# Five of six blocks of attention's value projection by seven quarter products, with the values kept in DRAM between

## The chip, the cores and the metric

One core of one Trainium2 chip runs a whole two-layer block in one launch. The metric is the device time of that launch in microseconds, as the median of several runs. The five engines are TensorE (PE, with its weight loads as PEld), VectorE (DVE), ScalarE (ACT), GpSimd (POOL) and SyncE (SP, which here only issues DMAs).

## The reference

512 tokens of width 1024 pass through two layers: an HGRN mixer with a SwiGLU FFN, and dilated attention with a SwiGLU FFN, each with normalisation and modulation. The change touches the second layer's attention. There one projection gives queries, keys and values for three dilation groups of eight heads of 128:

```python
proj = (u @ w_in).astype(jnp.float32).reshape(B, S, N_GROUPS, 3, ATT_HEADS, ATT_HEAD_DIM)
for gi, (window, dilation) in enumerate(DILATED_GROUPS):
    q = apply_partial_rope(proj[:, :, gi, 0], cos, sin) * scale
    k = apply_partial_rope(proj[:, :, gi, 1], cos, sin)
    v = proj[:, :, gi, 2]
    o_g, lse_g = dilated_group_attention(q, k, v, window, dilation)
```

So the values are three products of 512 x 1024 by 1024 x 1024. Each group attends in windows of 128 positions, group 0 over neighbouring tokens, groups 1 and 2 over every fourth and every sixteenth token; the groups' outputs are merged by a softmax over their log-sums and projected out. Everything is float32.

## The kernel before

**Products.** Float32 products are made from three products of fp32r parts (`three`, L415 to L419): each operand is split into a high part (an ACT cast) and a low part (a DVE subtraction), and high x high, high x low, low x high are added up in PSUM. The activations `u` of a layer lie split in `uh` and `ul`. A weight tile of 1 MB (128 x 2048) is loaded by SP into one of two `raw` buffers and split into one of three `hi` and `lo` buffers (class `Stream`, L84 and L85, or in two pieces, L105 and L106). The order of the loads is a list written out beforehand (`items`); `weave` puts pieces of the modulation (`ada`, eight DVE operations per vector half, L245) between the weights.

**The FFN's stage of seven products.** In both FFNs most of the first matrix is multiplied by quarters in the manner of Strassen and Winograd: operands are cut in four, and seven products of quarters with sums made on DVE and POOL replace eight (`token_sums`, `seven_products`, L726 to L881). There the sums of the tokens are made under two plain blocks.

**The attention's values.** A value block is one group and one half of the heads: 512 tokens by 1024 by 512 columns, made as four token tiles of 8 x 3 products of 512 columns. Six such blocks exist. The first, group 0 and heads 0 to 3, is multiplied inside `ffn(0, ...)`, at the end of the first layer: token tile by token tile between the last normalisations (`open_attention` returns `v_prod`; its ACT copy is L1532). Groups 1 and 2 of the first half follow (`tok_proj`), and those of the second half, with group 0, come after the queries and keys of head 4. For groups 1 and 2 the result goes through DRAM (`bounce`, L1343 and L1345, POOL's queue) to be read back with a stride of four tokens. The values stay in SBUF as `V[g]`, 512 columns at a time.

**The heads.** For every head and group a query and a key block (`block`, 24 products of 512 columns each) is multiplied; `fl` (class `Fillers`) runs scores, softmax, merging, flips and value products (`pv_r`, `pv_n`) of the earlier head between them at fixed half steps (`fl.tick`).

**What sets the order.** Outside marked blocks a scheduler orders each engine's queue by program order and readiness. Inside `with tc.manual_schedule(engines=ORDERED)` the queues of PE, ACT, DVE and POOL hold that block's operations in the order in which they are written; `ffn`'s end, from the last weight tiles on, is such a block. Engines run their own queues in order and wait for one another by semaphores. PSUM has eight banks: four tagged `mm`, two `a`, two `b`.

## Time and profile before

| | us |
|---|---|
| median of three runs | 1513.37 (1510.27 to 1513.59) |
| the profiled execution, its time | 1511.66 |
| its span from the first to the last instruction | 1509.9 |
| end of the first layer's FFN and first value block | 645 to 680 |
| two value blocks, then the heads | 680 to 1136 |
| mean granted TensorE clock | 0.997 of full speed |

A row of a timeline gives the start, the time taken, engine, line, operation, written tile `<-` read tiles, shape and count; in square brackets stands how long the engine had been idle before and whose end released it. Times are from the start of the span. A row by windows gives the stretch, its length, busy time and instructions of PE, PEld, DVE, ACT and POOL, the granted clock, the DMA share and GB/s. Matmuls are pipelined: their durations overlap, and the distance between starts is what one costs.

### The profile page before, as it was taken

To read this page: it belongs to the slowest core of one execution; us is meant where nothing else is said; L and a number is where in the kernel's file an instruction comes from. 1 tells how busy PE (TensorE), PEld (TensorE's weight loads), DVE (VectorE), ACT (ScalarE), POOL (GpSimd) and SP (SyncE) were. 2 spreads that over 40 slices of the span, in tenths; PEclk is the share of its full clock that TensorE was granted. 3 is DMA by queue.
4 is the path that set the end of the run, shared out by engine and by line. 5 is a ranking of instruction groups with operands and counts; after the bars stand their busy time and mean duration, and the time that the engine had idled before them with its cause. 6 is when DMAs were issued, how large, how long until landed. Compare 5 with 4: busy or idle time off the path is not lost.

```text
span 1509.9 us, 23161 instructions
## 1 busy us (share of the span) xinstructions
PE 1495.6 (99%) x9111; PEld 1307.1 (87%) x9111; DVE 1032.7 (68%) x1764; ACT 692.8 (46%) x1107; POOL 255.9 (17%) x232
## 2 busy tenths in 40 slices
...
GB/s 305 179 174 132 162 140 168 112 62 134 110 106 107 104 210 212 165 56 203 183 144 141 115 111 112 209 181 58 84 34 79 103 94 112 110 104 154 194 111 56
DMA packets 209502, 201.23 MB, mean 133 GB/s; under 512 B 7096, under 2 KB 167024, under 8 KB 208880
## 3 DMA queue, kind: packets, MB, share of 16 engines
...
q10 hardware_dynamic: 512, 0.35, 0.1%
...
## 4 chain that ended last, share of the span: by engine, by line
PE 87%; DVE 6%; POOL 2%; issue 2%; ACT 2%; DMA 1%; DVEq 0%; POOLq 0%; ACTq 0%; SPq 0%
PE ps_mm L417 19%; PE ps_mm L419 19%; PE ps_mm L418 19%; PE ps_b L417 3%; PE ps_b L419 3%; PE ps_b L418 3%; PE ps_a L419 3%; PE ps_a L417 3%; PE ps_a L418 3%; PE ps_mm L1165 1%; DVE loq L795 1%; POOL raw L775 1%; PE ps_a L1617 1%; PE ps_a L1165 1%; PE ps_mm L223 1%
## 5 line engine op out<-in xcount | busy, mean ns | idle before, releaser
L417 PE MATMUL ps_mm<-uh,hi 128*128 128x512 f32 (+1 forms) x784 | 290.2, 370 | 0.0
L419 PE MATMUL ps_mm<-uh,lo 128*128 128x512 f32 (+1 forms) x784 | 288.2, 368 | 0.0
L418 PE MATMUL ps_mm<-ul,hi 128*128 128x512 f32 (+1 forms) x784 | 287.3, 366 | 0.0
L85 DVE TENSOR_TENSOR lo<-raw,hi 128x2048 fp32r<-128x2048 f32 x74 | 174.5, 2358 | 149.0 <-ACT hi L84 148.8
L84 ACT CAST hi<-raw 128x2048 fp32r<-128x2048 f32 x74 | 141.4, 1911 | 155.1 <-DMA raw<-in_ffn_w_out_dram 50.8
L417 PEld LDWEIGHTS ps_mm<-uh,hi 128*128 128x128 f32 x784 | 147.4, 188 | 31.7 <-issue 8.4
L419 PEld LDWEIGHTS ps_mm<-uh,lo 128*128 128x128 f32 x784 | 147.6, 188 | 23.5
L418 PEld LDWEIGHTS ps_mm<-ul,hi 128*128 128x128 f32 x784 | 147.5, 188 | 22.5
L791 ACT CAST hiq<-raw 128x1024 fp32r<-128x1024 f32 x72 | 72.4, 1051 | 72.2 <-DVE raw L779 70.9
L417 PE MATMUL ps_mm<-hi,oh 128*128 128x512 f32 x240 | 94.0, 392 | 0.2 <-ACT oh L413 0.2
L418 PE MATMUL ps_mm<-lo,oh 128*128 128x512 f32 x240 | 93.6, 390 | 0.0
L245 DVE SCALAR_TENSOR_TENSOR shared<-raw,cond,shared 128x512 f32<-128x512 f32 x98 | 73.4, 749 | 27.7 <-DMA raw<-in_ada_w_dram 26.2
L795 DVE TENSOR_TENSOR loq<-raw,hiq 128x1024 fp32r<-128x1024 f32 x72 | 84.9, 1219 | 0.0
L775 POOL TENSOR_TENSOR raw<-raw 128x512 f32<-128x512 f32 x36 | 57.9, 1608 | 105.8 <-DVE loq L771 45.7
L419 PE MATMUL ps_mm<-hi,ul 128*128 128x512 f32 x192 | 74.9, 390 | 0.0
L418 PE MATMUL ps_mm<-lo,uh 128*128 128x512 f32 x192 | 74.7, 389 | 0.0
L417 PE MATMUL ps_mm<-hi,uh 128*128 128x512 f32 x192 | 73.4, 390 | 0.0
L779 DVE TENSOR_TENSOR raw<-raw 128x1024 f32<-128x1024 f32 x36 | 44.1, 1225 | 40.9 <-POOL raw L775 40.9
L419 PE MATMUL ps_mm<-hi,ol 128*128 128x512 f32 x176 | 68.5, 389 | 0.0
L825 POOL TENSOR_TENSOR shared<-shared 128x256 f32<-128x256 f32 x36 | 30.3, 840 | 206.1 <-DVE shared L824 206.1
L247 POOL PARTITION_ALL_REDUCE shared<-shared x12 | 40.6, 3380 | 133.6 <-DVE shared L245 123.7
L417 PE MATMUL ps_mm<-sums,hiq 128*128 128x256 f32 x216 | 59.7, 276 | 0.0
...
## 6 DMA issues: line engine op xcount, KB each, us to landing
raw<-in_ada_w_dram SPq DMA_DIRECT2D x40, 1024.0 KB, 5.1
...
raw<-in_ffn_w_out_dram SPq DMA_DIRECT2D x22, 1024.0 KB, 4.9
raw<-in_hgrn_w_in_dram SPq DMA_DIRECT2D x12, 1024.0 KB, 5.3
raw<-in_attn_w_in_dram SPq DMA_DIRECT2D x12, 1024.0 KB, 5.0
raw<-in_ffn_w_in_dram SPq DMA_DIRECT2D x8, 1024.0 KB, 5.0
...
```

The lines of the kernel that those rows point to most:

```text
L84: self.nc.scalar.copy(hi, t)
L85: self.nc.vector.tensor_sub(lo, t, hi.bitcast(F32))
L245: dve.scalar_tensor_tensor(a, r[:, k], sc, a, op0=OP.mult, op1=OP.add)
L247: pool.partition_all_reduce(a, a, P, bass.bass_isa.ReduceOp.add)
L417: pe.matmul(ps, ah, bh, start=start, stop=False)
L418: pe.matmul(ps, ah, bl, start=False, stop=False)
L419: pe.matmul(ps, al, bh, start=False, stop=stop)
L775: pool.tensor_add(r[:, 2], r[:, 2], r[:, 0])
L779: dve.tensor_tensor(r[:, 0:2], r[:, 0:3:2], r[:, 1:2].broadcast_to((P, 2, 512)), op=OP.add)
L791: act.copy(hi, src)
L795: dve.tensor_sub(lo, src, hi.bitcast(F32))
L825: pool.tensor_add(W[:, 3], W[:, 3], W[:, 5])
```

## The change

The first block (group 0, heads 0 to 3) stays plain, but its result goes to DRAM. The other five, the `UNITS`, are made directly after it, in a stage of their own (`values`) that continues the hand-ordered block at the end of `ffn(0, ...)`. Tokens, inner dimension and columns are each cut in two; seven products p1 to p7 of 256 tokens by 512 by 256 columns replace eight. The sums of token quarters (`full_sum`, `less`, `less_both`, `t_parts`: T0 to T3) are built in the first unit. Every unit sums its weight quarters (S1 on POOL, S2 to S4 on DVE), splits seven quarters, and adds the products up with two ACT copies, six DVE operations and one POOL operation. Its two weight tiles are loaded together, one into `raw`, one into a buffer of its own; the split parts use the `hi` and `lo` buffers. Each result of 1 MB is stored to a DRAM tile `vals[g, half]` from POOL's queue. The heads then fetch the values for two heads at a time, three loads from POOL's queue, with the stride of four tokens for groups 1 and 2; two sets of buffers are held. `tok_proj` and its `bounce` are gone, the pieces of the next weight tile at the end of `ffn` too, and the modulation pieces are woven in from the first head on, one per 1.6 items instead of one per 2.

```diff
--- before.py
+++ after.py
+TPAD = 112
...
+ADA_AT = (0, 1.6)
...
+    def load_unit(self, other):
+        i = self.loaded
+        if i < len(self.items) and self.items[i][0] == "unit":
+            first, second = self.items[i][1]
+            self.raw[i] = [self.pool.tile([P, 2048], F32, name=f"raw{i}", tag="raw", bufs=self.raws),
+                           other.tile([P, 2048], F32, name=f"other{i}", tag="other", bufs=2)]
+            for t, src in zip(self.raw[i], (first, second)):
+                self.nc.sync.dma_start(t.rearrange("p (a b) -> p a b", a=4), src)
+            self.loaded += 1
+    def unit(self):
+        assert self.items[self.done][0] == "unit"
+        self.done += 1
+        return self.raw.pop(self.done - 1)
     def fill(self):
...
-        while self.loaded < len(self.items) and sum(map(real, range(self.done, self.loaded))) + real(self.loaded) <= self.raws:
+        while self.loaded < len(self.items) and self.items[self.loaded][0] != "unit" and sum(map(real, range(self.done, self.loaded))) + real(self.loaded) <= self.raws:
...
+        UNITS = ((1, 0), (2, 0), (0, 1), (1, 1), (2, 1))
...
-        at = []
-        order = []
-        for hd in range(NH):
-            if hd == 0:
-                for g in range(3):
-                    order.append(("v", g, 0))
-                    at += av(g, 0)
-            for g in range(3):
-                order.append(("qk", g, hd))
-                at.append(aqk(g, hd))
-            if hd == 4:
-                for g in range(3):
-                    order.append(("v", g, 1))
-                    at += av(g, 1)
-        items += weave(at, ada_seq((1, 2), (1, 4), (1, 3)), 6, 2)
+        items += av(0, 0) + [("unit", [w for _, w in av(*unit)]) for unit in UNITS]
+        items += weave([aqk(g, hd) for hd in range(NH) for g in range(3)], ada_seq((1, 2), (1, 4), (1, 3)), *ADA_AT)
...
-                    for hi_f, lo_f in st.pieces(2, True):
-                        hi_f()
-                        lo_f()
-                    st.fill()
                     v_prod(vw, 2, range(8))
                     v_prod(vw, 3, range(8))
-                turns.close()
+                    turns.close()
+                    nxt[2]()
...
-        def tok_proj(dst, via=None, ticks=()):
-            ws = [st.take(), st.take(1)]
-            bounce = None if via is None else fresh(dpool, [S, 512], "bounce", 2)
-            for t in range(NT):
-                ps = bank("mm")
-                for kt in range(KT):
-                    whi, wlo = ws[kt // 4]
-                    w = slice((kt % 4) * 512, (kt % 4 + 1) * 512)
-                    three(ps, nat(uh[:, kt])[t], nat(ul[:, kt])[t], whi[:, w], wlo[:, w], kt == 0, kt == KT - 1)
-                if via is None:
-                    act.copy(dst[:, t], ps)
-                else:
-                    m = via[t % len(via)]
-                    act.copy(m, ps)
-                    pool.dma_start(bounce[t * P:(t + 1) * P], m)
-            if via is not None:
-                pool.dma_start(dst, bounce.rearrange("(l r) d -> l r d", r=4))
-                if t in ticks:
-                    fl.tick()
...
-        oT, V, store = [], [], []
         scr = dpool.tile([NH, 2, S, 2], F32, name="scr")
+        vals = {(g, hf): dpool.tile([S, 512], F32, name=f"vals{g}{hf}") for g in range(3) for hf in range(2)}
         heads = {}
         L4 = lambda a: a.rearrange("p (l r) -> p r l", r=4)
+        vx = ExitStack()
+        room_of = {}
+        def out_of(unit):
+            pool.dma_start(vals[unit].rearrange("(t p) d -> p t d", p=P), room_of[unit])
 
         def open_attention():
 
-            ctx.enter_context(hx)
-            otp = hx.enter_context(tc.tile_pool(name="a_ot", bufs=1))
-            oT.extend(heads_of(otp))
-            store.append(otp)
-            hx.enter_context(cx)
-            vp = cx.enter_context(tc.tile_pool(name="a_v", bufs=1))
-            V.extend(vp.tile([P, NT, 512], F32, name=f"V{g}") for g in range(3))
+            va = vx.enter_context(tc.tile_pool(name="a_val", bufs=1))
+            room_of["pool"] = va
             banks = {}
+            dst = room_of[0, 0] = fresh(va, [P, NT, 512], "vals", 2)
+            for _ in range(2):
+                st.load_unit(va)
...
-                    act.copy(V[0][:, t], banks[t])
+                    act.copy(dst[:, t], banks[t])
...
+        def values():
+            va = room_of["pool"]
+            vb = vx.enter_context(tc.tile_pool(name="a_sums", bufs=1))
+            sums_t = vb.tile([P, TPAD + 8 * 1024], F32R, name="sums_a")[:, TPAD:]
+            K4 = lambda t: t.rearrange("p (k n) -> p k n", k=4)
+            Q = lambda t, c: t.rearrange("p (k n) -> p k n", k=4)[:, :, c * 256:c * 256 + 256]
+            H2 = lambda a: a.rearrange("p (a n) -> p a n", a=2)
+            th, tl = [[K4(sums_t[:, o + k:o + k + 1024]) for k in range(0, 4096, 1024)] for o in (0, 4096)]
+            rooms = [vb.tile([P, NT, 512], F32, name="room_a"), fresh(va, [P, NT, 512], "vals", 2)]
+            full = [K4(r.rearrange("p a n -> p (a n)")[:, o:o + 1024]) for r in rooms for o in (0, 1024)]
+            u_of = lambda r, c: [tuple(x[:, 4 * r + k, c * 256:c * 256 + 256] for x in (uh, ul)) for k in range(4)]
+            t_of = lambda i: [(th[i][:, k], tl[i][:, k]) for k in range(4)]
+            US = {"p1": u_of(0, 0), "p2": u_of(1, 0), "p3": u_of(1, 1),
+                  "p5": t_of(0), "p7": t_of(1), "p4": t_of(2), "p6": t_of(3)}
+            def full_sum(k, eng):
+                a = [x[:, 4 * (k // 2):4 * (k // 2) + 4, k % 2 * 256:k % 2 * 256 + 256].bitcast(F32) for x in (uh, ul)]
+                eng.tensor_add(full[k], *a)
+            def less(k, a, b):
+                dve.tensor_sub(full[k], full[a], full[b])
+            def less_both(k, a, b):
+                dve.scalar_tensor_tensor(full[k], full[a], -1.0, full[b], op0=OP.mult, op1=OP.subtract)
+            def t_parts(k):
+                split(th[k], tl[k], full[k])
+            class Unit:
+                def __init__(self, which):
+                    self.which = which
+                    self.steady = which != UNITS[0]
+                    raw = st.unit()
+                    self.q1, self.q0, self.q3, self.q2 = (Q(r, c) for r in raw for c in range(2))
+                    s1 = fresh(va, [P, 1024], "s1", 1)
+                    self.s1 = K4(s1)
+                    self.n = 0
+                    self.at, self.bank = {}, {}
+                def S1(self):
+                    pool.tensor_add(self.s1, self.q0, self.q2)
+                def S3(self):
+                    dve.tensor_add(self.q0, self.q0, self.q1)
+                def S2(self):
+                    dve.tensor_add(self.q1, self.s1, self.q1)
+                def S4(self):
+                    dve.tensor_add(self.q3, self.q3, self.q1)
+                def parts(self, p):
+                    src = {"p1": self.q1, "p2": self.q3, "p3": self.q3, "p4": self.q2, "p5": self.s1, "p6": self.q1,
+                           "p7": self.q0}[p]
+                    if self.n % 2 == 0:
+                        self.tiles = st.part_tiles()
+                    o = self.n % 2 * 1024
+                    self.n += 1
+                    self.at[p] = [t[:, o:o + 1024] for t in self.tiles]
+                    split(*(K4(x) for x in self.at[p]), src)
+                def hold(self):
+                    self.dst = room_of[self.which] = fresh(va, [P, NT, 512], "vals", 2)
+                def run(self, p):
+                    ps = self.bank[p] = bank("a" if p == "p3" and not self.steady else "mm")
+                    hi, lo = self.at.pop(p)
+                    for s in range(2):
+                        tok = slice(s * P, s * P + P)
+                        o = ps[:, s * 256:s * 256 + 256]
+                        for kt in range(4):
+                            w = slice(kt * 256, kt * 256 + 256)
+                            uhi, ulo = US[p][kt]
+                            three(o, uhi[:, tok], ulo[:, tok], hi[:, w], lo[:, w], kt == 0, kt == 3)
+                def to(self, c, r):
+                    return self.dst[:, 2 * c:2 * c + 2, 256 * r:256 * r + 256]
+                def keep2(self):
+                    self.w2 = fresh(va, [P, 512], "w2", 1)
+                    act.copy(self.w2, self.bank["p1"])
+                def keep3(self):
+                    self.w3 = fresh(va, [P, 512], "w3", 1)
+                    act.copy(self.w3, self.bank["p5"])
+                def add4(self):
+                    self.w4 = fresh(va, [P, 512], "w4", 1)
+                    dve.tensor_add(self.w4, self.w2, self.bank["p6"])
+                def add5(self):
+                    self.w5 = fresh(va, [P, 512], "w5", 1)
+                    dve.tensor_add(self.w5, self.w4, self.bank["p7"])
+                def add1(self):
+                    self.w1 = fresh(va, [P, 512], "w1", 1)
+                    pool.tensor_add(self.w1, self.w4, self.w3)
+                def out11(self):
+                    dve.tensor_add(self.to(0, 0), H2(self.w2), H2(self.bank["p2"]))
+                def out12(self):
+                    dve.tensor_add(self.to(1, 0), H2(self.w1), H2(self.bank["p3"]))
+                def out21(self):
+                    dve.scalar_tensor_tensor(self.to(0, 1), H2(self.w5), -1.0, H2(self.bank["p4"]), op0=OP.mult, op1=OP.subtract)
+                def out22(self):
+                    dve.scalar_tensor_tensor(self.to(1, 1), H2(self.w5), -1.0, H2(self.w3), op0=OP.mult, op1=OP.subtract)
+                    out_of(self.which)
+            a = Unit(UNITS[0])
+            a.S1()
+            out_of((0, 0))
+            a.parts("p1")
+            a.parts("p2")
+            full_sum(3, pool)
+            full_sum(2, pool)
+            a.S3()
+            a.S2()
+            a.S4()
+            full_sum(0, dve)
+            full_sum(1, dve)
+            less(0, 0, 1)
+            a.parts("p3")
+            a.parts("p5")
+            t_parts(0)
+            a.hold()
+            a.run("p1")
+            less(1, 3, 1)
+            less_both(3, 0, 3)
+            a.keep2()
+            a.run("p3")
+            t_parts(3)
+            a.parts("p6")
+            less_both(2, 3, 2)
+            a.run("p2")
+            t_parts(2)
+            a.run("p5")
+            a.parts("p4")
+            a.out11()
+            t_parts(1)
+            a.keep3()
+            a.run("p6")
+            a.parts("p7")
+            st.load_unit(va)
+            b = Unit(UNITS[1])
+            b.S1()
+            a.add4()
+            a.add1()
+            b.parts("p1")
+            a.run("p4")
+            b.S3()
+            b.S2()
+            a.run("p7")
+            b.parts("p6")
+            a.out12()
+            b.parts("p5")
+            a.add5()
+            for n in range(1, len(UNITS)):
+                last = a
+                a, b = b, None
+                a.hold()
+                a.run("p1")
+                a.parts("p2")
+                last.out21()
+                a.run("p6")
+                a.S4()
+                a.keep2()
+                last.out22()
+                a.parts("p7")
+                a.run("p5")
+                a.parts("p3")
+                a.add4()
+                a.run("p2")
+                a.keep3()
+                a.add1()
+                a.parts("p4")
+                st.load_unit(va)
+                if n + 1 < len(UNITS):
+                    b = Unit(UNITS[n + 1])
+                    b.S1()
+                else:
+                    st.fill()
+                a.run("p7")
+                a.out11()
+                if b:
+                    b.parts("p1")
+                    b.S3()
+                a.run("p3")
+                a.add5()
+                if b:
+                    b.S2()
+                    b.parts("p6")
+                a.run("p4")
+                a.out12()
+                if b:
+                    b.parts("p5")
+            a.out21()
+            a.out22()
+            vx.close()
...
+        ffn(0, first, h0.close, ((1, 0), open_attention, values), "right")
+        ctx.enter_context(hx)
+        otp = hx.enter_context(tc.tile_pool(name="a_ot", bufs=1))
+        oT = heads_of(otp)
+        hx.enter_context(cx)
+        vp = cx.enter_context(tc.tile_pool(name="a_v", bufs=1))
+        V = {}
+        def fetch(pair):
+            if pair < NH // 2:
+                V[pair] = [fresh(vp, [P, NT, 256], f"V{g}", 2) for g in range(3)]
+                for g in range(3):
+                    src = vals[g, pair // 2][:, pair % 2 * 256:pair % 2 * 256 + 256]
+                    pool.dma_start(V[pair][g], src.rearrange(*(("(l r) d -> l r d",) if g else ("(t p) d -> p t d",)),
+                                                             **({"r": 4} if g else {"p": P})))
...
-            hs = slice((hd % 4) * P, (hd % 4 + 1) * P)
+            hs = slice((hd % 2) * P, (hd % 2 + 1) * P)
...
+            if hd % 2:
+                fetch(hd // 2 + 2)
         fl.n = 0
-        for kind, g, i in order[1:]:
-            if kind == "v":
-                tok_proj(V[g], None if g == 0 else oT[5:] if i else oT[4 * g - 4:4 * g], (0, 1, 2) if i and g == 0 else ())
-                continue
+        for pair in range(2):
+            fetch(pair)
+        for i, g in ((hd, g) for hd in range(NH) for g in range(3)):
...
-        first = mixer_out(oT, store[0], (3, 5), gates.pop((1, 2)), 1, "left", cx.close, tail)
+        first = mixer_out(oT, otp, (3, 5), gates.pop((1, 2)), 1, "left", cx.close, tail)
```

13 lines of the change are left out of this document (6 added, 7 removed).

## The prediction, made before the result was known

> **What bounds the kernel now.** I read the page first: busy shares and the chain that ended last.
>
> ```profile
> PE 1495.6 (99%) x9111; PEld 1307.1 (87%) x9111; DVE 1032.7 (68%) x1764; ACT 692.8 (46%) x1107; POOL 255.9 (17%) x232
> PE 87%; DVE 6%; POOL 2%; issue 2%; ACT 2%; DMA 1%; DVEq 0%; POOLq 0%; ACTq 0%; SPq 0%
> ```
>
> TensorE is busy 99% of 1509.9 us and 87% of the chain. A busy share is an average, so I asked for the stretch that the change rewrites (the attention heads from the second value block on), for one head with modulation work beside it and one without, and for whom PE waits at all.
>
> ```profile
> 686.00:1130.00 444.00, 443.76 (x2198) 375.67 (x2198) 258.21 (x682) 225.52 (x373) 53.06 (x58) 1.00 0.44 131
> 785.52:825.89 40.37, 40.37 (x213) 34.53 (x211) 31.97 (x95) 27.54 (x47) 3.96 (x6) 1.00 0.43 119
> 1054.48:1095.56 41.08, 41.08 (x216) 35.10 (x214) 23.84 (x73) 23.77 (x42) 2.63 (x4) 1.00 0.25 78
> PE ps_b L500 <- DVE xn L494: 2.6, 2, 1.6
> ```
>
> The columns after the length are busy PE, PEld, DVE, ACT, POOL. PE has no hole in 444 us. The longest wait for an engine outside the first microseconds is 1.6 us, once. So here a PE microsecond saved is a microsecond of the kernel, and a PE microsecond lost is one too: there is no old idle time for either to vanish in.
>
> **What the products save.** A plain block is 4 token tiles x 8 x 3 = 96 products of 512 columns. A block by seven products is 7 x 2 token tiles x 4 x 3 = 168 products of 256 columns. The timeline of PE gives the pitch of the first. The second shape already runs in the FFN's stage of seven products, 84 products to a round; POOL's sum at L775 comes once in each round and shows its length.
>
> ```profile
> 722.54 0.39 PE L417 MATMUL ps_mm<-uh,hi 128*128 128x512 f32 x1
> 722.77 0.39 PE L418 MATMUL ps_mm<-ul,hi 128*128 128x512 f32 x1
> 723.00 0.39 PE L419 MATMUL ps_mm<-uh,lo 128*128 128x512 f32 x1
> 432.66 1.62 POOL L775 TENSOR_TENSOR raw<-raw 128x512 f32<-128x512 f32 x1 [1.77 <-DVE spare L771]
> 442.33 1.62 POOL L775 TENSOR_TENSOR raw<-raw 128x512 f32<-128x512 f32 x1 [1.77 <-DVE loq L771]
> 451.99 1.62 POOL L775 TENSOR_TENSOR raw<-raw 128x512 f32<-128x512 f32 x1 [1.77 <-DVE spare L771]
> ```
>
> Starts lie 0.227 us apart, so a plain block takes 96 x 0.2267 = 21.76. A round of 9.665 us is 0.115 per product, so a block by seven takes 168 x 0.115 = 19.32. Five blocks save 5 x 2.44 = 12.2 us if PE never waits. Half of the 512 pitch (0.1133) would make it 13.6; a pitch of 0.1175 would make it 10.1.
>
> **What the seven products ask of the other engines.** Each block needs three weight sums of 1024 columns on DVE, one on POOL, seven splits (a 1024 cast on ACT, a 1024 subtraction on DVE), and seven more adds of 512 (six on DVE, one on POOL) plus two ACT copies. The token sums (four full sums, three differences, four splits) are built once, inside the first block. Prices:
>
> ```profile
> 349.77 4.62 DVE L739 TENSOR_TENSOR sums<-mid,sums 128x1024 fp32r<-128x1024 f32 x4
> 347.02 2.00 ACT L738 CAST sums<-mid 128x1024 fp32r<-128x1024 f32 x2 [12.07 <-DVE mid L735]
> 439.83 0.69 DVE L830 TENSOR_TENSOR shared<-shared,ps_b 128x512 f32<-128x512 f32 x1
> 440.44 1.75 DVE L771 TENSOR_TENSOR loq<-raw,hiq 128x1536 fp32r<-128x1536 f32 x1
> 670.18 1.30 POOL L518 TENSOR_TENSOR ul<-u,uh 128x512 fp32r<-128x512 f32 x1 [0.57 <-ACT uh L517]
> L1345 POOL DMA_DIRECT2D V<-bounce x4: 542/551/556, 705.1 to 992.1; - x4
> L795 DVE TENSOR_TENSOR loq<-raw,hiq x72: 1214/1218/1227, 360.9 to 1373.3; 128x1024 fp32r<-128x1024 f32 x72
> ```
>
> Four DVE operations of 1024 take 4.62 and one alone 1.22, so each adds (4.62 - 1.22) / 3 = 1.13. A DVE add of 512 adds 0.6 (the next one starts 0.61 after 439.83). ACT needs 1.0 for a cast of 1024 (two in 2.00). POOL's 512 is 1.25 to 1.3, so a POOL sum of 1024 is about 2.4 (estimate, doubled less its start). A DMA issue holds POOL 0.55.
>
> **A price that the shares hide.** POOL and DVE do not run such sums side by side:
>
> ```profile
> 670.18 2.56 POOL L518 TENSOR_TENSOR ul<-u,uh 128x512 fp32r<-128x512 f32 x2 [0.57 <-ACT uh L517]
> 671.61 2.21 DVE L106 TENSOR_TENSOR lo<-raw,hi 128x1024 fp32r<-128x1024 f32 x1 [1.85 <-ACT hi L105]
> 439.81 0.74 POOL L825 TENSOR_TENSOR shared<-shared 128x256 f32<-128x256 f32 x1 [5.53 <-DVE shared L824]
> ```
>
> POOL's pair ends at 672.74. DVE's subtraction starts at 671.61 and takes 2.21 instead of 1.22: it ends 1.08 after POOL does, as if nothing had been done before. L830 above, with one operand in PSUM, ran its usual 0.69 beside POOL's L825. So I price a DVE operation with two SBUF operands as waiting until POOL's sum has ended. A reading in which the two only share bandwidth would cost about half of the 6.8 us below, and the sum would be +5 instead of +8.5. The Trainium skill, "SBUF - State Buffer", section "SBUF: two separate sides", calls the shared pair "an exclusive lock, not a bandwidth split" for just these operations; the 2.21 agrees.
>
> **The first block by seven: the term that decides.** All of it lies within a hand-ordered block, and so do the plain block's products and copies ahead of it. In such a block each engine keeps the written order; the trace shows ACT doing so, with only work from outside the block (L84) slipped in:
>
> ```profile
> 673.78 0.59 ACT L1532 COPY V<-ps_mm 128x512 f32<-128x512 f32 x1 [1.25 <-PE ps_mm L419]
> 676.50 1.92 ACT L84 CAST hi<-raw 128x2048 fp32r<-128x2048 f32 x1 [2.13 <-PE ps_mm L419]
> 679.67 0.59 ACT L1532 COPY V<-ps_mm 128x512 f32<-128x512 f32 x1 [1.26 <-PE ps_mm L419]
> 679.25 0.39 PE L419 MATMUL ps_mm<-hi,ul 128*128 128x512 f32 x1
> ```
>
> The last copy comes when PE has finished the plain block: 0.2 us after PE could have begun a next product (679.25 + 0.23). After it in ACT's order comes the cast for p1; DVE's first operation of the stage is the subtraction behind that cast, so DVE, though it has been idle, can begin none of its sums earlier. On POOL the order is first weight sum, then the issue of the finished plain block's store (which waits for the same last copy), then two of the full token sums, then the next block's weight sum. So everything starts when PE runs dry. Up to the last product p7 DVE's queue holds 21 operations: p1, p2, three weight sums, two full sums, a difference, p3, p5, T0, two differences, T3, p6, a difference, T2, p4, an output add, T1, p7. That is 20 x 1.13 + 0.6 = 23.2 us. To it come:
> - that 0.2, the copy 0.5 and p1's cast 1.0, with handoffs: 1.8;
> - POOL's three sums that stand before DVE: the first is granted at the end of the 0.55 issue, 0.4 before p1's subtraction asks, and holds it 2.0; the other two 2.4 each: 6.8;
> - two gaps in which DVE waits for ACT's cast of a token sum it has just made (T3, T2), 1.1 each: 2.2;
> - p7 itself on PE, 24 x 0.115 = 2.7 after its parts.
>
> Sum 23.2 + 1.8 + 6.8 + 2.2 + 2.7 = 36.7 us for a block whose products are 19.3: PE stands still 17.4 us. The order p1, p3, p2 costs nothing by itself, since DVE's queue sets the end.
>
> **The second block** starts with DVE behind: after p7's parts come an add, p1, POOL's add (1.25), two sums, a gap of 1.1 for p6's cast, and p6: 0.6 + 1.13 + 1.25 + 2.26 + 1.1 + 1.13 = 7.5 us, while PE has p7 and p1, 5.4, to do: about 2 us lost, and 1.4 more at p5, whose bank is freed only by the old block's third output. Together 3.4. **Blocks three to five:** DVE has 10 x 1.13 + 6 x 0.6 = 14.9 us of its own, POOL's two sums stand before it for up to 3.65, and one cast gap is 1.1: at most 19.6 against PE's 19.3. The adds from PSUM run beside POOL, so I take 0, with 1 us for all three as the upper end.
>
> **Moved and removed work.**
>
> ```profile
> raw<-in_attn_w_in_dram SPq DMA_DIRECT2D x12, 1024.0 KB, 5.0
> L245 DVE SCALAR_TENSOR_TENSOR shared<-raw,cond,shared 128x512 f32<-128x512 f32 x98 | 73.4, 749 | 27.7 <-DMA raw<-in_ada_w_dram 26.2
> 682.10 2.29 DVE L85 TENSOR_TENSOR lo<-raw,hi 128x2048 fp32r<-128x2048 f32 x1 [1.36 <-ACT hi L84]
> ```
>
> The bounce of strided values through DRAM (16 stores and 4 loads on POOL's queue) becomes 6 stores and 12 loads of 0.55 us; the 12 loads, 3 per two heads, are wanted ten half steps later. A load waits for the last value products of the pair before, and behind it in POOL's queue are the small statistics DMAs; the 20 now there cost PE nothing, so 0, with 1 us if one load blocks them. Weights: a load of 1 MB lands in 5.0 us, and the first two units are asked for as soon as the FFN's room is free, with the plain block's 21.76 us still ahead: 0. Modulation now begins with the first head and comes every 1.6 items instead of every 2: per head 3 / 1.6 - 3 / 2 = 0.4 more pieces of 4 x 0.75 us and a finish of about 1, so DVE 31.97 + 1.6 of 40.4: 83%, 0. Handing over to the first head: its weight split (ACT 1.9, DVE 2.3) can slip into the last block as L84 did above; 0, but 4 us if it is queued behind the last two outputs.
>
> **The clock.** Idle PE has a second price. Columns as before, granted clock third from the end:
>
> ```profile
> 9.00:12.00 3.00, 1.23 (x17) 0.30 (x17) 1.21 (x4) 2.50 (x6) 0.55 (x1) 1.00 1.05 390
> 13.00:16.00 3.00, 2.08 (x12) 2.02 (x11) 2.07 (x8) 2.82 (x7) 1.34 (x3) 0.50 1.17 312
> 16.00:19.00 3.00, 2.98 (x12) 2.29 (x11) 2.90 (x5) 1.29 (x4) 1.00 (x1) 0.50 1.12 339
> ```
>
> After PE had been busy 1.23 of 3 us the clock was 0.5 for the next two windows. Before p3, PE waits 5 us at one stretch and 3 more after a first product, so I expect one such stretch of 0.5. During it PE still waits for DVE, so a slow p3 and p2 cost nothing; if 0.5 held through the second block it would add 6.6. The Trainium skill, "TensorE: Matmul & The Clock Gate", Part 1, gives half rate after "≥1 idle window"; by that rule the clock falls here too, which changes the clock column and not the sum.
>
> **Sum.** Stalls 17.4 + 3.4 = 20.8, less 12.2: +8.6 us. The profiled execution took 1511.66, so 1520.2 by this sum; it lay 1.7 under the median of the three runs, 1513.37, to which the forecast applies: 1522.
>
> **Rivals.**
> 1. *The sums do not meet* (17%). If POOL's sums fall where DVE waits anyway, the 6.8 and most of the second block's loss vanish: the same walk ends at +0.5, 1513.9. For it: POOL's operations lie in DVE's gaps all through the FFN. Against it: here DVE has no gaps.
> 2. *Preparation begins under the plain block* (20%): ACT and POOL take the first casts and the two full sums before the last copy and the store. DVE was idle then, and 7 us of its queue move under the plain block's last products. With the holding by POOL the walk gives +3.3 (1516.7), without it -6.9 (1506.5): the other side. It decides from 4 us of head start if POOL never holds DVE. Against it stands the written order.
> 3. *DVE sets the pace of every block, or the clock stays down* (10%): at 1.22 per 1024 operation instead of 1.13 the walk gives +12.7 (1526); 0.5 through the second block, +15.1 (1528.5).
> 4. *The seven products are not denser than plain ones* is excluded by the FFN's rows, down to the 10.1 above.
>
> **Numbers.** The forecast has 53%, its own range +5 to +12 (1518 to 1525), from the bandwidth reading, the pitch, and the handing over. The range reaches to rivals 1 and 2, mostly, and to the lower end of 3: 1508 to 1528. About 0.3%, 4.5 us, is what a measurement of this kernel can tell from no change. Faster by more: rival 2 without holding and something for an order that I misread, 0.18. Within: rival 1, the rest of 2 and the low edge of the forecast, 0.28. Slower: 0.54.
>
> **What would show it.** In the changed profile: PE waits for DVE right after the plain block, over 10 us in all and in one stretch over 4, and the first block lasts 33 to 39 us; DVE subtractions of 2 us and more where a POOL sum runs; three later blocks of 19.3 with PE dense; heads of 41 us as now; a clock under 1.00 near 690 us. It is wrong if DVE works on token sums before the plain block's last copy, if PE's total wait in the stage is under 12 us, or if heads get longer.

## The result and the profile after

The changed kernel took 1537.49 us (median of four runs, 1534.75 to 1538.27) beside 1512.54 us for the kernel before on the same chip: a ratio of 1.0164, 95% interval 1.0146 to 1.0182. It is slower by 25 us. The forecast was 1522 with a range of 1508 to 1528: the sign was right, the size was not.

The profile's page after, its busy shares and its chain by engine:

```profile
PE 1495.1 (97%) x9471; PEld 1322.2 (86%) x9471; DVE 1108.8 (72%) x1843; ACT 705.0 (46%) x1125; POOL 287.1 (19%) x242
PE 85%; DVE 6%; DMA 3%; ACT 2%; issue 2%; POOL 1%; SPq 0%; POOLq 0%; DVEq 0%; ACTq 0%
```

PE by windows, as in the prediction: about the first unit, the second, the third, and the heads.

```profile
680.10:719.00 38.90, 26.23 (x176) 25.11 (x176) 34.75 (x24) 13.33 (x15) 11.15 (x5) 0.82 0.21 76
719.00:741.00 22.00, 20.68 (x173) 20.27 (x172) 17.74 (x19) 8.69 (x10) 6.26 (x3) 1.00 0.46 154
741.00:760.00 19.00, 19.00 (x167) 19.00 (x165) 15.56 (x16) 7.98 (x10) 6.22 (x3) 1.00 0.49 166
799.00:1160.00 361.00, 350.60 (x1777) 298.40 (x1776) 242.76 (x679) 202.03 (x349) 52.01 (x55) 0.99 0.47 135
```

A hole is a stretch in which PE runs no product. PE, which had none in 444 us before, has them in two places: 12.7 us of the first window's 38.9 and 1.3 us of the second's 22, and 10.4 us of the heads' 361. The units from the third on are dense. By PE's timelines (of the profiled runs) the 25 us split so:

| part | before | after | difference | predicted |
|---|---|---|---|---|
| five value blocks / the stage of seven products | 108.8 | 118.3 | +9.5 | +8.6 |
| the heads and the output projection, value blocks left out | 374.5 | 389.1 | +14.6 | 0 |
| everything else | | | +1 | 0 |

The second row runs from the first query product (722.5 before, 798.4 after) to the first product of the last FFN (1162.3 and 1187.6); of before's 439.8 us, 65.3 are the three value blocks that stood between the heads (3 x 21.76). So the forecast's sum held where it was worked out, and the miss is the step that was set to nothing.

**The stage.** Whom PE waits for there (in all, times, longest):

```profile
PE ps_mm L426 <- DVE loq L422: 7.7, 3, 5.8
PE ps_a L426 <- DVE loq L422: 3.2, 1, 3.2
PE ps_mm L425 <- ACT hiq L421: 2.1, 2, 1.6
PE ps_a L425 <- ACT hiq L421: 1.0, 1, 1.0
```

The timeline at its start (ACT, DVE, POOL), then DVE and POOL 18 us later:

```profile
680.32 0.59 ACT L1520 COPY vals<-ps_mm 128x512 f32<-128x512 f32 x1 [4.85 <-PE ps_mm L427]
680.80 1.05 ACT L421 CAST hiq<-raw 128x1024 fp32r<-128x1024 f32 x1
681.88 6.17 DVE L422 TENSOR_TENSOR loq<-raw,hiq 128x1024 fp32r<-128x1024 f32 x1 [11.03 <-ACT hiq L421]
681.21 1.07 POOL L1501 DMA_DIRECT2D vals<-vals  x1 [5.07 <-ACT vals L1520]
682.32 4.64 POOL L1542 TENSOR_TENSOR vals<-uh,ul 128x1024 f32<-128x1024 f32 x2
699.70 3.40 DVE L1545 TENSOR_TENSOR room_a<-vals,room_a 128x1024 f32<-128x1024 f32 x1
698.73 3.29 POOL L1567 TENSOR_TENSOR s<-raw,other 128x1024 f32<-128x1024 f32 x1 [11.76 <-DVE loq L422]
```

This is the predicted picture: after the last plain copy the cast for p1, DVE idle for 11 us until then, and DVE's first subtraction at 6.17 us instead of 1.22. It ends at 688.05, 1.1 after POOL's two full sums (686.96).

**The heads.** Whom PE waits for there:

```profile
PE ps_a L1810 <- ACT qk L1789: 5.5, 1, 5.5
PE ps_a L1828 <- ACT qk L1789: 3.2, 1, 3.2
PE ps_b L1912 <- ACT pt L1881: 1.7, 1, 1.7
```

The first of these waits, from PE's row back, on the timeline (PE; DVE's end of the rotation, the positional turning of queries and keys; ACT):

```profile
826.82 0.58 PE L1810 MATMUL ps_a<-qk,qk 128*128 128x128 f32 x1 [5.53 <-ACT qk L1789]
815.08 0.68 DVE L1786 TENSOR_TENSOR turning<-turning,rot 64x512 f32<-64x512 f32 x1
823.71 1.90 ACT L103 CAST hi<-raw 128x2048 fp32r<-128x2048 f32 x1 [12.97 <-DMA raw<-in_attn_w_in_dram]
```

The weight load in front of it, in the chain of waits (the split of an earlier weight, the load's issue, the load):

```profile
807.03 2.30 DVE lo L104
809.35 0.37 SPq L66
809.77 13.84 DMA raw<-in_attn_w_in_dram
```

The DMA issues between 798 and 827 (count, size of each, median us to landing):

```profile
raw<-in_attn_w_in_dram SPq DMA_DIRECT2D x6, 512.0 KB, 10.2
V<-vals POOLq DMA_DIRECT2D x6, 512.0 KB, 8.4
```

And that stretch by windows (clock, DMA share and GB/s at the end):

```profile
812.00:827.00 15.00, 9.47 (x43) 7.53 (x42) 5.11 (x8) 3.26 (x4) 4.19 (x3) 0.95 1.06 312
```

PE's first score products stand 5.5 us. They need queries that ACT copies after the rotation (L1789). DVE had finished that rotation at 815.8, but ACT stood in front of a weight cast for 13 us, with the copies behind it in its queue. The weights took 13.84 us, in a stretch where the DMA engines are full (share 1.06): the first values of two pairs of heads (`V<-vals`, 3 MB) and a modulation load issued at 804.5 are under way with them. The weight load was also issued late: weights and modulation take turns in two tiles, and the chain goes back to the split that freed one of them at 809.3.

### The profile page after: what moved, and what is told of

The parts are those of the page before. It is cut to its first block, busy times and chain, and to the rows that moved or that the text cites. A ratio compares the mean times of both kernels' runs of the same rounds, so it can differ in the third digit from the quotient of the medians.

```text
span 1535.3 us, 24027 instructions
## 1 busy us (share of the span) xinstructions
PE 1495.1 (97%) x9471; PEld 1322.2 (86%) x9471; DVE 1108.8 (72%) x1843; ACT 705.0 (46%) x1125; POOL 287.1 (19%) x242
## 4 chain that ended last, share of the span: by engine, by line
PE 85%; DVE 6%; DMA 3%; ACT 2%; issue 2%; POOL 1%; SPq 0%; POOLq 0%; DVEq 0%; ACTq 0%
PE ps_mm L425 18%; PE ps_mm L426 18%; PE ps_mm L427 18%; PE ps_b L426 3%; PE ps_b L425 3%; PE ps_b L427 3%; PE ps_a L425 3%; PE ps_a L427 3%; PE ps_a L426 3%; PE ps_mm L1170 1%; DMA raw<-in_attn_w_in_dram 1%; DVE loq L422 1%; PE ps_a L1810 1%; PE ps_a L1828 1%; PE ps_a L1170 1%
## 5 line engine op out<-in xcount | busy, mean ns | idle before, releaser
L104 DVE TENSOR_TENSOR lo<-raw,hi 128x2048 fp32r<-128x2048 f32 x65 | 152.6, 2348 | 97.9 <-ACT hi L103 97.9
L103 ACT CAST hi<-raw 128x2048 fp32r<-128x2048 f32 x65 | 124.1, 1909 | 158.2 <-DMA raw<-in_ffn_w_out_dram 60.1
L264 DVE SCALAR_TENSOR_TENSOR shared<-raw,cond,shared 128x512 f32<-128x512 f32 x98 | 73.3, 748 | 20.4 <-DMA raw<-in_ada_w_dram 18.6
L783 POOL TENSOR_TENSOR raw<-raw 128x512 f32<-128x512 f32 x36 | 57.9, 1608 | 107.2 <-DVE loq L779 45.7
L425 PE MATMUL ps_mm<-sums,hiq 128*128 128x256 f32 x216 | 59.7, 277 | 0.7 <-DVE mid L909 0.7
L426 PE MATMUL ps_mm<-sums,hiq 128*128 128x256 f32 x216 | 59.7, 276 | 0.0
L427 PE MATMUL ps_mm<-sums,loq 128*128 128x256 f32 x216 | 59.7, 276 | 0.0
L425 PE MATMUL ps_a<-hi,oh 128*128 128x512 f32 x152 | 59.6, 392 | 0.0
```

Of the source, the lines that this page charges most:

```text
L103: self.nc.scalar.copy(hi, t)
L104: self.nc.vector.tensor_sub(lo, t, hi.bitcast(F32))
L264: dve.scalar_tensor_tensor(a, r[:, k], sc, a, op0=OP.mult, op1=OP.add)
L425: pe.matmul(ps, ah, bh, start=start, stop=False)
L426: pe.matmul(ps, ah, bl, start=False, stop=False)
L427: pe.matmul(ps, al, bh, start=False, stop=stop)
```

## The experiments

Every run is beside the kernel before on the same chip. The chips differ between groups of runs, and the medians of the kernel before on them lie between 1511.4 and 1513.1, so times of different groups compare to about 2 us. The table gives what the sections below refer to: the stage (from the last plain product ahead of the seven products to the first query product; where two plain blocks are made, both but the first counted), the heads as defined above, in them the holes of PE over 0.6 us, and the time at half clock (a granted clock of 0.5). All but the medians are from the profiled run.

| run | median us | ratio (95%) | stage | heads | holes | half clock |
|---|---|---|---|---|---|---|
| after | 1537.5 | 1.0146-1.0182 | 118.3 | 389.1 | 5.9, 0.8, 3.7, 2.0 | 10.2 |
| e1_plain_stage | 1526.6 | 1.008-1.011 | 109 | 387.9 | 3.1, 4.3, 2.0, 1.9 | 6.8 |
| e2_fetch_later | 1533.7 | 1.0128-1.0159 | 118.3 | 385.6 | 0.9, 5.1, 1.4, 2.0 | 6.8 |
| e3_pool_sums_first | 1529.7 | 1.0105-1.0136 | 113.2 | 387.5 | 6.5, 0.8, 3.7, 2.0 | 6.8 |
| e4_sums_under_plain | 1531.7 | 1.0109-1.0143 | 111.5 | 391.6 | 7.6, 0.8, 3.8, 2.0 | 13.7 |
| e5_mod_sparser | 1531.5 | 1.0111-1.0147 | 118.3 | 383.8 | 6.0, 0.8, 2.0 | 6.8 |
| e6_mod_no_loads | 1526.1 | 1.0077-1.0107 | 118.3 | 380.1 | 2.0, 0.8, 0.9, 2.0 | 0 |
| e7_mod_one_product | 1534.1 | 1.0131-1.0162 | 118.3 | 387.6 | 8.1, 0.8, 1.2, 2.0 | 10.2 |
| e8_all_sums_dve | 1527.3 | 1.0085-1.0123 | 109.7 | 391.4 | 7.4, 0.8, 3.7, 2.0 | 13.7 |
| e9_mod_second_head | 1540.3 | 1.0159-1.0204 | 118.3 | 393.8 | 1.1, 3.1, 4.1, 2.2, 1.1, 1.4, 2.0 | 13.7 |
| e10_mod_moved | 1531.5 | 1.0106-1.0136 | 118.3 | 379.3 | 1.2, 1.7, 2.0 | 0 |
| e11_unit_started_early | 1526.7 | 1.0065-1.0108 | 106.6 | 391.6 | 7.3, 0.8, 4.0, 2.0 | 13.7 |
| e12_all | 1518.2 | 1.0023-1.0054 | 106.6 | 378.5 | 1.6, 0.8, 2.0 | 0 |
| e13_no_fetch | 1532.8 | 1.0126-1.0155 | 118.3 | 386.1 | 1.8, 0.7, 5.8, 2.0 | 6.8 |
| e14_two_plain | 1512.9 | 1.0002-1.0019 | 99.8 | 379.9 | 1.8, 1.6, 2.0 | 0 |
| e15_third_slot | 1535.1 | 1.0144-1.0171 | 118.5 | 387.1 | 3.2, 1.3, 0.8, 0.7, 1.8, 2.0 | 6.8 |
| e16_two_plain_third_slot | 1518.1 | 1.0027-1.0055 | 99.8 | 390.3 | 3.9, 1.3, 1.2, 1.5, 0.7, 1.8, 2.0 | 6.8 |
| e17_mod_clear_of_fetch | 1533.2 | 1.012-1.0147 | 118.4 | 384.4 | 1.5, 4.5, 0.7, 2.0 | 3.4 |
| e18_two_plain_clear | 1513.5 | 0.9995-1.0016 | 99.8 | 388.6 | 1.8, 4.7, 1.0, 0.7, 1.4, 2.0 | 6.8 |

A hole is taken from the start of one product to the start of the next. The holes account for the heads' length in every row: 374.5 plus the holes gives it to within 0.4 us where the clock stayed full, and with half clock it lies up to 4.4 us above that (after: 374.5 + 12.3 = 386.8 of 389.1).

### Which half of the change makes the heads longer: e1, e2

The theory at this point was that the heads' loss is the traffic of fetches and loads there (A); the rivals, that it is a late result of the disturbed stage (B), or comes from the modulation's start with the first head (C).

**e1_plain_stage**: the five units by plain products at the same place, outside the hand-ordered block, and the pieces of the next weight tile back at the end of `ffn`.

```diff
-        items += av(0, 0) + [("unit", [w for _, w in av(*unit)]) for unit in UNITS]
+        items += av(0, 0) + [w for unit in UNITS for w in av(*unit)]
...
-            a = Unit(UNITS[0])
...
+            for unit in UNITS:
+                ws = [st.take(), st.take(1)]
...
+                    act.copy(dst[:, t], ps)
+                out_of(unit)
```

> The changed kernel with the five units made by plain products (96 of 512 columns) in the same place, everything else as changed: values to DRAM, loads for two heads at a time, heads without value blocks between them, modulation from the first head on. Theory A: the loss has two places, the start of the seven products (PE waits 20 us, 9.6 net of their saving) and the first heads, where six value loads of 0.5 MB at once hold up a weight load (13.8 us instead of 5) and with it ACT's queue (14.7 us). Then this kernel loses only the second: 1512.5 + 14.7, so 1525 to 1529, five plain blocks in 108.8 us with PE dense, and the same wait of about 8 us for ACT near the first scores. Rival B: the loss in the heads is a late result of the disturbed value stage (DVE behind, clock down). Then it is gone here: 1511 to 1516. Neither gives anything at 1537.

1526.6 us: the stage is dense at 109 us, and the heads are still 13.4 longer than before's. Rival B falls: the seven products account for 1.2 of the 14.6 us at most. The rest comes from what was moved: values in DRAM, no value block between the heads, modulation from the first head on. The wait of about 8 us expected near the first scores did not come in that form: the holes are 3.1 us at 840 and 4.3 us at 878.

**e2_fetch_later**: the first two pairs of values are fetched behind head 0's and head 1's statistics.

```diff
+                    if pair < 2:
+                        tc.keep_in_program_order(ins)
...
-        for pair in range(2):
-            fetch(pair)
         for i, g in ((hd, g) for hd in range(NH) for g in range(3)):
+            if i < 2 and g == 2:
+                fetch(i)
```

> The changed kernel with the first two pairs' value loads pinned in POOL's queue behind the statistics store of heads 0 and 1 instead of all six at once at the start of the heads. Theory A: the first heads' waits (8.6 us near the first scores, part of the 4.7 us at the next head, 3 to 5 us of half clock) go: 9 to 14 us faster than the changed kernel, 1524 to 1529; the value stage stays at 118 us and the weight loads land in 5 to 8 us. Rival C: the heads lose because modulation is woven in from the first item and no value block lies between them, and DVE and ACT cannot follow; then at most 3 us change, 1534 to 1538.

1533.7: less than 4 us came back, more than rival C allowed and far less than the 9 to 14 of theory A. The hole of 5.9 us at 821 did not vanish, it went with the fetch to 848:

```profile
853.27 0.58 PE L1830 MATMUL ps_a<-qk,qk 128*128 128x128 f32 x1 [4.75 <-ACT qk L1791]
```

### What the heads wait for: e5, e6, e7, e9, e13

**e6_mod_no_loads** and **e7_mod_one_product** take the modulation in the heads apart: e6 leaves its twelve 1 MB loads out and keeps DVE's work, e7 keeps the loads and leaves three of four products out.

```diff
# e6
+        items = [("ada", None, it[2]) if it[0] == "ada" and i >= after_values else it for i, it in enumerate(items)]
...
-                r = V4(raw)
+                r = [cs[:, 0]] * 4 if raw is None else [V4(raw)[:, k] for k in range(4)]
# e7
+                    if l == 1 and v > 1 and v < 5 and k:
+                        continue
```

> As after, but the twelve 1 MB loads of the modulation in the heads are left out: its products read a tile that lies in SBUF anyhow, so DVE's and POOL's work for it stays as it is. Theory A (DVE stands in front of late modulation loads, the rotation behind it): heads 374 to 380, time 1522 to 1529. Theory B (DVE's own work is too much): heads 386 to 390, time 1534 to 1538. Theory C (the two fetches of values, or POOL's all-reduce, which holds DVE): heads 384 to 390, time 1532 to 1538.

> As after, but in the heads each modulation chunk is multiplied with one of its four pieces: three of four products are left out, 36 on DVE at about 0.75 us, 27 us in all; the loads, the waits for them and the sums over partitions stay. Theory A: DVE waits for the same loads at the same places, heads 384 to 389, time 1532 to 1538. Theory B (DVE's own work): heads 374 to 380, time 1522 to 1529. Theory C (fetches or all-reduce): heads 385 to 390, time 1533 to 1538.

e6 took 1526.1 us and its heads 380.1 (theory A's 374 to 380, within 0.1); the two long holes and every half clock are gone. e7 took 1534.1, heads 387.6, with the first hole at 8.1: 27 us less work for DVE bought 1.5 us in the heads. The loads bind; DVE's work has a part only in the second hole, which shrank from 3.7 to 1.2. Why the first grew, no run tells.

**e13_no_fetch** leaves the fetches out and keeps the modulation.

```diff
+                if pair:
+                    V[pair] = V[0]
+                    return
...
                 for g in range(3):
+                    pool.memset(V[pair][g], 0.0)
+                    continue
```

> As after, but the heads fetch no values: the tiles of the first pair are set to zero on POOL before the heads and serve all pairs (24 loads of 0.5 MB left out, the stores of the values stay). Theory D (the first stall is the meeting of the fetches with the first modulation and weight loads): the gap of 5.9 us at 821 goes to under 2, its half clock with it; the stall of 3.7 us at 890, which has no fetch beside it, stays; heads 380 to 384, time 1529 to 1533. Rival E (the modulation loads at a cold start do it alone): the gap stays at 4 to 6 us, heads 386 to 389, time 1534 to 1538. If the gap of 2 us near 1135 goes too, it was the late fetches.

1532.8. (The loads left out are 12, not 24.) No hole at 821; the same loads between 798 and 827 land in half the time (DMA issues of this run):

```profile
raw<-in_attn_w_in_dram SPq DMA_DIRECT2D x6, 512.0 KB, 4.8
```

Whom PE waits for in its heads:

```profile
PE ps_a L1833 <- ACT qk L1794: 6.7, 2, 5.3
PE ps_b L1917 <- ACT pt L1886: 1.7, 1, 1.7
```

So the first hole needs both: without modulation loads (e6) it is gone though the fetches run and the weights land late (median 9.1 us), without fetches (e13) it is gone though the modulation runs. It is a meeting. What the modulation load adds to it, its bytes or its turn in the two tiles, these runs do not separate: with no modulation between them (e6) the weights are also issued earlier (timeline of SP):

```profile
785.61 14.07 SPq L66 DMA_DIRECT2D raw<-in_attn_w_in_dram  x6
```

Theory D was right on that hole; the heads' total, 386.1 against an expected 380 to 384, was not, because the second hole grew to 5.8. The hole of 2 us near the end stays: it is not the fetches.

**e5_mod_sparser** and **e9_mod_second_head** change only the weaving.

```diff
# e5
-ADA_AT = (0, 1.6)
+ADA_AT = (0, 2)
# e9
-ADA_AT = (0, 1.6)
+ADA_AT = (3, 1.5)
```

> As after, but in the heads one group of the modulation's items follows every 2 weights (after: every 1.6; before: every 2). Nothing is left out. In after the eight heads take 389.2 us where before's took 374.5. Theory A (DVE, which works its queue in order, stands in front of a modulation load that lands late, and the rotation of the next queries and keys waits behind it): sparser loads collide less, heads 378 to 385, time 1527 to 1534. Theory B (DVE's own time for the modulation is too much between the heads' steps): much the same, 1527 to 1534. Rival C (the values' way through DRAM and the cold start of the weights, which this edit does not touch): heads 387 to 390, time 1535 to 1538.

> As after, but the heads' modulation starts with the second head's weights, one group every 1.5 weights, so the first head has no modulation load; nothing is left out. Theory A1 (the loss is a collision at the hand-over: the stream of weights starts cold there, and the first modulation load takes the place and the bandwidth that the first head's weights need): the gap of 5.9 us at 821 and its half clock go, heads 380 to 385 in place of 389.2, time 1528 to 1533. Theory A2 (modulation loads of this density stall DVE's queue wherever they start): the gap moves into the second head, heads 387 to 390, time 1535 to 1538.

e5: 1531.5. The second hole is gone, the first (the meeting) is not: 6.0. e9: 1540.3, slower than after. The meeting is gone (1.1 at 831), but at one group every 1.5 weights DVE and PE now stop at 860, 887 and 935. A1 held for the place; the time and the heads lie above even A2's ranges. Start and density changed together here, so the run does not tell which of them made the new holes.

How the second hole arises, in after (the timeline of DVE, then POOL, ACT and PE):

```profile
881.81 1.54 DVE L264 SCALAR_TENSOR_TENSOR shared<-raw,cond,shared 128x512 f32<-128x512 f32 x2 [3.91 <-DMA raw<-in_ada_w_dram]
883.27 2.28 DVE L104 TENSOR_TENSOR lo<-raw,hi 128x2048 fp32r<-128x2048 f32 x1
887.22 0.73 DVE L264 SCALAR_TENSOR_TENSOR shared<-raw,cond,shared 128x512 f32<-128x512 f32 x1
888.48 2.72 DVE L1785 TENSOR_TENSOR turning<-turning,shared 64x512 f32<-64x512 f32 x1
888.05 3.60 POOL L266 PARTITION_ALL_REDUCE shared<-shared  x1 [5.45 <-DVE shared L264]
891.96 2.23 ACT L1789 COPY qk<-turning 32x512 f32<-32x512 f32 x2 [4.54 <-DVE turning L1786]
894.24 0.58 PE L1828 MATMUL ps_a<-qk,qk 128*128 128x128 f32 x1 [3.19 <-ACT qk L1789]
```

DVE stands 3.9 us before a modulation load; then the held-up products, a weight's split and the rotation come at once; and beside the sum over partitions that the last product releases on POOL the rotation's multiplication takes 2.72 us where 0.68 is usual. PE gets its operands 3.2 us late. e6, with every one of these steps but the wait for the load, has at most 2.0 there.

### More room or another place: e10, e15, e17

**e10_mod_moved**: one of the three vectors under the first FFN's second matrix, the others from the second head, every 2 weights.

```diff
-ADA_AT = (0, 1.6)
+ADA_AT = (3, 2)
...
-        items += weave(f0b[:9], ada_seq((1, 1), (1, 0)), 0, 0.9) + f0b[9:]
+        items += weave(f0b[:9], ada_seq((1, 1), (1, 0), (1, 4)), 0, 0.7) + f0b[9:]
...
-        items += weave([aqk(g, hd) for hd in range(NH) for g in range(3)], ada_seq((1, 2), (1, 4), (1, 3)), *ADA_AT)
+        items += weave([aqk(g, hd) for hd in range(NH) for g in range(3)], ada_seq((1, 2), (1, 3)), *ADA_AT)
```

> As after, but one of the three modulation vectors of the heads is made under the second matrix of the first feed-forward block instead (14 groups there in place of 10), and the other two start with the second head, one group every 2 weights; nothing is left out. Theory A (modulation loads among the heads' weights): heads 376 to 380 in place of 389.2, feed-forward block at most 2 us longer, time 1524 to 1529. Rival (the work costs the same wherever it stands): the second matrix gets longer by what the heads gain, time 1532 to 1538.

The heads did what was expected, 379.3; the FFN took about 2.3 us back (the plain block ends at 682.4 instead of 680.1, with new holes of 1.3 us at 622 and 669): 1531.5, above the 1524 to 1529 expected.

**e15_third_slot**: three tiles for the loads in the heads.

```diff
...
+        if self.extra and i < self.upto and self.turn % 3 == 1:
+            t = self.extra.tile([P, 2048], F32, name=f"rawx{i}", tag="rawx", bufs=1)
+        else:
+            t = self.pool.tile([P, 2048], F32, name=f"raw{i}", tag="raw", bufs=2)
...
```

> As after, but in the heads the loads of weights and modulation go through three 1 MB tiles in turn in place of two; nothing is left out or moved. Theory F (the ring of two is the bound: a modulation load can't start before the item two ahead of it has been worked off, and DVE, ACT and in the end PE stand before it): the loads run one item further ahead, the stalls of 5.9 and 3.7 us and their half clocks go, heads 376 to 381 in place of 389.2, time 1524 to 1529. Rival G (what is short is bandwidth where loads and fetches meet, or DVE's own time): heads 385 to 390, time 1533 to 1538.

1535.1, heads 387.1, in rival G's ranges: theory F falls as stated. The long holes became six short ones. It does not test the start well: the third tile's first load was issued only at 800.3, behind the values' stage, and ACT's cast of it began at 809.5, at the end of the hole of 3.2 us.

**e17_mod_clear_of_fetch**: the start at the third weight, every 2 weights, nothing moved.

```diff
-ADA_AT = (0, 1.6)
+ADA_AT = (2, 2)
```

> As after, but the heads' modulation starts at the third weight, when the first fetches have landed, and has a group every 2 weights as in before; the last three groups then stand behind the heads' last weight. Nothing is left out. Theory H (meeting of fetch and modulation, and density, are the whole loss but for 2 us near the end): no stall over 2 us, heads 377 to 380 in place of 389.2, time 1525 to 1529. Rival (without value blocks between the heads the modulation does not fit among them at any place): stalls of 3 to 4 us elsewhere, or a wait at the output projection for the last groups, heads 383 to 389, time 1531 to 1537.

1533.2, heads 384.4, in the rival's ranges. The meeting is gone (1.5 at 836), but a hole of 4.5 us stands at 885, at before's density. Theory H falls for the second hole: density alone does not set it. e5, with the same density and the groups two weights earlier, has none, and e2, which moves only the fetches, has 1.4 there; which coincidence of load, sum over partitions and rotation decides, no run tells.

### The first unit: e3, e4, e8, e11

**e3_pool_sums_first**: the store of the plain block is issued behind the two full sums, so that POOL makes them under the plain block. **e4_sums_under_plain**: the whole first part of `values` ahead of the plain block's last two tiles. **e8_all_sums_dve**: the same, with the full sums on DVE. **e11_unit_started_early**: also S1 on DVE, the first parts one tile earlier, and p2 ahead of p3.

```diff
# e3
             a.S1()
-            out_of((0, 0))
...
             full_sum(2, pool)
+            out_of((0, 0))
# e4
+                    turns.close()
+                    rest = nxt[2]()
+                    next(rest)
                     v_prod(vw, 2, range(8))
                     v_prod(vw, 3, range(8))
-                    turns.close()
-                    nxt[2]()
+                    for _ in rest:
+                        pass
...
             a.S1()
-            out_of((0, 0))
...
             less(0, 0, 1)
+            yield
+            out_of((0, 0))
# e8, on top of e4
-            full_sum(3, pool)
-            full_sum(2, pool)
+            full_sum(3, dve)
+            full_sum(2, dve)
```

> The changed kernel with one line moved: on POOL the store of the plain block is issued behind the two full token sums instead of ahead of them, so the sums run near 676 while PE is still in the plain block and DVE waits. Theory A (a POOL sum stops DVE subtractions for its whole length): p1's subtraction takes 1.2 us instead of 6.2, and the stage is 4.5 to 5 us shorter, 113 us; 1532 to 1534 in all. Rival D (DVE and POOL only share bandwidth, and p1's 6.2 us come from something else, as the issue of the store): the stage gains under 2 us, 1536 or more.

> The changed kernel with the first unit's sums written ahead of the last two plain token tiles: the first weight sum, the splits of p1 and p2, the weight sums on DVE, the four full token sums and the first difference; the store and the rest stay behind. Theory A (the written order makes all preparation start when PE runs dry): DVE and POOL do 9 and 3 of their operations between 673 and 681, PE starts p1 at once, the first unit takes 20 to 25 us instead of 39, and the stage 99 to 106 us instead of 118: 12 to 19 us faster than the changed kernel, 1518 to 1526. Rival E (the start is bound by loads of the units or by PSUM banks, which stay as they are): under 5 us, 1532 or more.

> The fourth experiment (the first unit's sums and first parts ahead of the last two tiles of the plain block, the store of that block behind them), and with it the two full sums that POOL made are DVE's, so that only S1 is left on POOL there. If POOL's sums are what ate the head start (each stops a DVE instruction for its 3.3 us): DVE needs eleven instructions of 1.2 us, 13 to 15 us, in place of the 24 us seen; the stage of 118.3 us falls to 100 to 105 and the time to 1519 to 1524. Rival (the rest of the first unit is late whatever POOL does, since its casts and sums follow one on another): the stage stays at 109 to 112, time 1529 to 1532.

> As the eighth run (first unit ahead of the plain block's last two tiles, no full sum on POOL), and with it S1 on DVE too and with the first parts ahead of the plain block's second tile, and the second product taken before the third. If POOL's additions and the place in the order are all that holds the first unit: stage 99 to 105 us in place of 118.3 (eighth run 109.6), time 1520 to 1525 with heads as in after. Rival (the sums of the tokens can't start before the norm's last quarter is split at 674, and they follow one on another): stage 106 to 110, time 1526 to 1530; or the norm's tail is held up by the unit's work and the plain block ends later.

e3 took 5.1 us out of the stage, the size of the hold it removes; its time, 1529.7, lies below the 1532 to 1534 expected, and its heads are 1.6 shorter too. e4 had expected 12 to 19 and got 6.8 in the stage and 5.8 in all, and under the plain block three DVE operations in a row met a POOL operation (timeline of e4, DVE and POOL):

```profile
674.42 3.42 DVE L422 TENSOR_TENSOR loq<-other,hiq 128x1024 fp32r<-128x1024 f32 x1
677.75 3.41 DVE L1573 TENSOR_TENSOR raw<-raw 128x1024 f32<-128x1024 f32 x1
681.20 3.29 DVE L1576 TENSOR_TENSOR raw<-s,raw 128x1024 f32<-128x1024 f32 x1
673.35 3.40 POOL L1570 TENSOR_TENSOR s<-raw,other 128x1024 f32<-128x1024 f32 x1
676.71 6.70 POOL L1545 TENSOR_TENSOR vals<-uh,ul 128x1024 f32<-128x1024 f32 x2
```

Three operations of 1.22 took 10.1. Without POOL's two full sums (e8) the stage is 109.7, above the 100 to 105 expected and in the rival's range: taking them off POOL is worth 1.8 us there; with everything of e11 it is 106.6, as its rival said. So 9.1 us above dense PE (5 x 19.5 = 97.5) remain. The token sums read the low parts of the last tokens, which POOL finishes at 674.2 in e8, shortly before the stage; that this is what remains is read from the rows and was not tried by itself.

### Both together, and a version with two plain blocks: e12, e14, e16, e18

**e12_all** is e10 with e11. **e14_two_plain** is e10 with two plain blocks and four units, the first unit being prepared under the second plain block, with its S1 on DVE and p2 ahead of p3:

```diff
-        UNITS = ((1, 0), (2, 0), (0, 1), (1, 1), (2, 1))
+        UNITS = ((2, 0), (0, 1), (1, 1), (2, 1))
...
-        items += av(0, 0) + [("unit", [w for _, w in av(*unit)]) for unit in UNITS]
+        items += av(0, 0) + av(1, 0) + [("unit", [w for _, w in av(*unit)]) for unit in UNITS]
...
+            plain(0)
+            full_sum(3, dve)
+            full_sum(2, dve)
+            a = Unit(UNITS[0])
+            a.S1()
+            a.parts("p1")
+            a.parts("p2")
+            plain(1)
...
+            plain(3)
+            out_of((1, 0))
...
```

**e16_two_plain_third_slot** has the two plain blocks with e15's third tile, **e18_two_plain_clear** with e17's weaving; neither moves a vector.

> The edits of the tenth and the eleventh run together. If the two losses are separate places and add: heads 376 to 381, stage 99 to 105, time 1508 to 1515, about before's 1512. If the first unit's early work or the moved vector collides: 1516 to 1522.

> As the tenth run (one modulation vector moved, the others from the second head), and with two plain blocks and four units of seven products: the first unit's sums and parts are made under the second plain block, with no sum on POOL there. By the rows: stage behind the first plain block 21.8 + 4 x 19.3 = 99 us, with small waits 100 to 103, against 108.8 in before and 116.4 in the tenth run; heads 378 to 380; start 2 to 3 us later (the moved vector): time 1511 to 1516, within about 0.3% of before's 1512. If the second plain block's own weights or the first unit's steps come late (the weights of both follow one another through two tiles): stage 106 to 110, time 1518 to 1523.

> Two plain blocks and four units of seven products, three tiles for the loads in the heads, the modulation where after has it; nothing is left out. By the parts: stage 99 to 100 us (109 in before), heads 376 to 381 (374.5 in before), the first feed-forward block as in before: time 1504 to 1510, faster than before's 1512. By rival G: heads 385 to 390, time 1513 to 1518.

> The same edit in the kernel with two plain blocks and four units of seven products, first feed-forward block as in before; nothing is left out. By the parts: stage 99.7 us against 108.8 in before (9 less), heads 377 to 380 against 374.5 (3 to 5 more): time 1505 to 1509, 0.2 to 0.5% faster than before. By the rival: heads 383 to 389, time 1511 to 1517.

e12: 1518.2. The two losses are separate places and their repairs add: by the ratios e10 takes 0.43% off the changed kernel and e11 0.78%, and e12, with both, 1.25%. The time lies above the 1508 to 1515 expected since the stage is e11's 106.6, not 99 to 105, and the FFN holds the moved vector. e14: 1512.9, in the range expected, with a ratio of 1.0002 to 1.0019: level with before to 0.2%. (The stage of e10, which its expectation gives as 116.4, is 118.3.) Its second plain block and its four units, by windows:

```profile
686.40:708.00 21.60, 21.60 (x98) 17.90 (x97) 17.46 (x15) 6.03 (x8) 1.07 (x1) 1.00 0.28 98
708.00:786.00 78.00, 78.00 (x674) 78.00 (x673) 65.69 (x64) 36.20 (x39) 21.64 (x11) 1.00 0.46 144
```

PE has no hole in them: the stage is 9.0 us shorter than before's five blocks. The gain goes back in the heads (+5.4) and in the FFN, which holds the moved vector and ends some 6 us later (the second plain block starts at 686.1; holes of 1.1, 1.8, 1.0 and 1.3 us between 602 and 673). e16 took 1518.1: its stage is the expected one, 99.8, but its heads are 390.3, as rival G said, with a first hole of 3.9 us where ACT waits for the third tile's first load, as in e15. e18 keeps the FFN and has 0.9995 to 1.0016, not the 0.2 to 0.5% gain expected: in its profiled run the heads hold a hole of 4.7 us and are 388.6 long, as its rival said. Its runs lie between 1509.1 and 1516.2; the profile is of one at 1516.1. No version here is measurably faster than the kernel before.

## Why the prediction was wrong in size, step by step

- **Products.** 0.115 us was predicted for a product of 256 columns; e14's four units (77.96 us by PE's timeline, 672 products) give 0.116. A block saves 2.27, not 2.44. Nearly right.
- **The units.** 36.7 for the first, 22.7 for the second and 3 x 19.3 = 57.9 for the rest were predicted. PE by windows, the first from the end of the plain block, the others from the first product of their unit (168 products to a unit; the last window holds units three to five):

```profile
680.10:718.19 38.09, 25.42 (x170) 24.30 (x169) 33.94 (x24) 13.33 (x15) 11.14 (x5) 0.82 0.20 69
718.19:739.88 21.69, 20.37 (x171) 19.96 (x169) 18.25 (x19) 7.91 (x9) 6.27 (x4) 1.00 0.50 171
739.88:798.44 58.56, 58.56 (x507) 58.56 (x505) 51.40 (x52) 25.15 (x27) 13.53 (x8) 1.00 0.45 140
```

Above a dense unit's 19.5 the first takes 18.6 us and the second 2.2, where 17.4 and 3.4 were predicted. That both sums are 20.8 is luck: the first term was 1.2 too small and the second 1.2 too large. Mechanism and place are as written: ACT's copy, p1's cast, DVE's queue, POOL's hold. The hold cost 7.1 us (6.17 and 3.40 against 1.22 each) where 6.8 was predicted, but not in the order expected: POOL kept it at p1 across two sums in a row, so that one operation paid 5 us in place of 2.0. The stage: +9.5 against +8.6, and the 0.9 is the products' price.
- **The half clock in the first unit** was said to cost nothing, because PE would wait for DVE anyway, and that held. The clock was 0.5 in two stretches of 6.83 us, from 685.6 and from 695.8, where one was expected, and the 176 products of the first window above, 20.4 us at 0.116, kept PE busy for 26.2. But after the clock was back PE caught up with DVE and stood before it again (timeline of DVE, then PE):

```profile
711.23 1.22 DVE L422 TENSOR_TENSOR loq<-other,hiq 128x1024 fp32r<-128x1024 f32 x1
712.50 0.38 PE L426 MATMUL ps_mm<-loq,sums_a 128*128 128x256 f32 x1 [1.05 <-DVE loq L422]
```

So the 5.8 us are not on top of PE's holes, they fill them: 12.7 us of holes in place of the 17.4 predicted.
- **Rivals.** The sums met (1 falls); DVE did nothing ahead of the last plain copy (2 falls); e3 and e4 show that, put there by hand, such preparation would have brought 5 to 7 us. DVE did not set the pace of every block, and the clock did not stay down through the second unit (1.00 in its window), so 3 falls too; what the clock cost, about 2 us, lay in the heads, which the rival did not have.
- **The step that failed** is "Moved and removed work", which set the heads to 0: "the 20 now there cost PE nothing, so 0, with 1 us if one load blocks them" for the fetches, "0" for the weights, and for the modulation "DVE 31.97 + 1.6 of 40.4: 83%, 0". They cost 14.6 us together, 13.4 of it without any seven products (e1); longer heads were one of the prediction's own signs of being wrong. The modulation was priced by DVE's busy share, the very average that the prediction's first paragraph warns of. What binds is the landing of a load in front of an engine that works in order: DVE stands 3.9 us before a modulation load with the rotation behind it, ACT 13 us before a weight load with the rotation's copies behind it, and PE has no other work then. The fetches were priced by their place in POOL's queue, and not as 3 MB that share the DMA engines with the weights (4.8 us to landing without them, 10.2 with them).
- **What the 14.6 us are made of.** Shown: the meeting of fetch and first modulation loads (a hole of 5.9 and its half clock; gone in e6, e9, e10, e13 and e17, present in e3, e4, e5, e7, e8 and e11, and moved by e2; e15 and e16, with three tiles, have an earlier hole of 3.2 and 3.9 us instead); the late modulation loads further on (3.7 and its half clock; gone in e6, which has no such loads, and in e5). Not caused by either: 2.0 us near 1135, in every run with the new heads. There ACT's queue has the rotation's copies ahead of the copy that PE waits for; before has them the other way round. The timeline of ACT, after:

```profile
1134.45 2.25 ACT L1789 COPY qk<-turning 32x512 f32<-32x512 f32 x2
1136.61 0.57 ACT L1881 COPY pt<-ps_a 128x512 f32<-128x512 f32 x1
```

and before:

```profile
1110.53 0.64 ACT L1670 COPY pt<-ps_a 128x512 f32<-128x512 f32 x1
1111.19 2.25 ACT L1578 COPY qk<-turning 32x512 f32<-32x512 f32 x2
```

That the order alone makes these 2 us was read from the rows and not tried.
- **Open:** what decides whether the second hole appears (e5 and e17 differ only in where the groups stand), whether the modulation load makes the first by its bytes or by its turn in the two tiles, and how much the value blocks between the heads protected the kernel before: no run put them back there beside the values in DRAM.
